# Retention's gate and stored values: two heads in one pass, 512 moving columns in place of 256

## The chip, the cores and the metric

The kernel runs on one core of one Trainium2 chip. The metric is device time in microseconds, the median of several runs. One further execution was recorded by the hardware profiler; its views are what the rows below come from.

## The reference

One decoder block over 1024 tokens of width 1024, in float32. Everything starts from one projection of the normed input, whose columns are cut into the parts that the two mixers need:

```python
h = rmsnorm(x, norm_mix)
proj = h @ w_in
(rq, rk, rv, rg, nq, kcr, vcr, ksl, vsl, kwn, vwn, ngate, ga, gb) = jnp.split(proj, split_at, axis=-1)
y_a = retention(rq, rk, rv, rg, gn_g) @ w_ret_o      # 4 heads, keys of 128, values of 256
y_b = nsa(nq, kcr, vcr, ksl, vsl, kwn, vwn, ngate, ...) @ w_nsa_o   # 8 heads, 3 branches
x = x + (sigmoid(ga) * y_a + sigmoid(gb) * y_b) @ w_out
x = x + conv_ffn(rmsnorm(x), ...)
return rmsnorm(x)
```

Inside `retention`, `rg` is the gate (`silu(g)` times the normed output, 256 columns for each of four heads) and `rv` the values (256 columns for each head).

## The kernel before

All products are float32 made of three passes: `split` writes a rounded copy (`hi`, on ScalarE, L129) and the rest (`lo`, on VectorE, L130), and `mm3` (L132 to L135) issues hi x hi, hi x lo and lo x hi into one PSUM bank. The normed input stands transposed in SBUF as `hT`, eight k slices of 128 by 1024 tokens.

`weights` (L140) loads a part of `w_in` into one of three raw buffers (`wraw`) by a transfer on SyncE's queue, and splits it into one of four pairs of buffers (`wsp`, tags `wh` and `wl`). Each buffer holds 128 x 1024 elements.

Two kinds of projection run beside attention. `stored` (L529) computes 128 channels of the merge gates for all tokens, with the weights stationary and 512 tokens of `hT` moving: 48 matmuls of 512 columns, one weight buffer. `ret_block` (L537) computes one head's 256 columns of retention's gate (`rg`) or values (`rv`), with 128 tokens of `hT` stationary and the 256 columns of the weights moving: two weight parts of four k slices each, 8 token tiles x 8 k x 3 = 192 matmuls of 256 columns. Two token tiles share a bank of PSUM, which ScalarE copies out in one instruction (`ge`, L549) and stores to scratch memory (L550).

Attention is 16 units of 128 queries and one group of heads (`unit`, L380), from the last queries to the first, each with scores, masks, exponentials, transposes and products with the values. Behind each unit the program puts one `stored` block, behind every fourth unit one gate block, and behind the last unit the value blocks of heads 0 and 1 (`SPILL_V` is 2). The framework's scheduler puts the instructions of each engine into a fixed order before the run, with the program's order as priority, and hands out buffers from the pools; so the projections fill TensorE wherever attention has nothing ready. In the trace they run ahead of the units beside which they are written. PSUM gives two banks to the projections (`mm`).

Behind this stage comes retention, head by head: query and key projections with two banks of `mm`, the stored gate loaded back (L641), for heads 0 and 1 the stored values loaded back (L660) into raw buffers, for heads 2 and 3 the values projected in place (L672 to L682). Then come the output projections, the merge and the feed-forward network, which the change does not touch.

Of the kernel before, what the change touches and what calls it, by code (L numbers as in the profile page):

```python
# [12 lines left out]
AF = mybir.ActivationFunctionType  # L13
# [5 lines left out]
P = 128  # L19
S = 1024  # L20
D = 1024
NT = S // P
KD = D // P
H_R = 4
DV = 256
# [11 lines left out]
C_RQ, C_RK, C_RV, C_RG = 0, 512, 1024, 2048  # L37
# [3 lines left out]
SPILL_V = 2  # L41
SPILL_Q = 0
# [42 lines left out]
def tile_hybrid_block(ctx: ExitStack, tc: tile.TileContext, x, norm_mix, w_in, ret_gn_g,  # L85
# [4 lines left out]
    nc = tc.nc  # L90
    x, out = x[0], out[0]
    w_in, w_ret_o, w_nsa_o, w_out = w_in[0], w_ret_o[0], w_nsa_o[0], w_out[0]
# [10 lines left out]
    def bank(tag, shape=(P, 512)):  # L103
        return psum.tile(list(shape), F32, name="ps_" + tag, tag=tag, bufs=banks[tag])


    def scratch(name, n, shape):
        return [dram.tile(list(shape), F32, name=f"{name}{i}") for i in range(n)]
# [6 lines left out]
    rv_scr = scratch("rv_scr", SPILL_V, (S, DV))  # L115
    rq_scr = scratch("rq_scr", SPILL_Q, (P, S))
    rg_scr = scratch("rg_scr", H_R, (S, DV))
# [10 lines left out]
    def split(hi, lo, src):  # L128
        nc.scalar.activation(hi, src, AF.Copy)  # L129
        nc.vector.tensor_sub(lo, src, f32(hi))  # L130

    def mm3(ps, ah, al, bh, bl, start, stop, more=False):  # L132
        nc.tensor.matmul(ps, ah, bh, start=start, stop=False, skip_group_check=more)  # L133
        nc.tensor.matmul(ps, ah, bl, start=False, stop=False, skip_group_check=more)  # L134
        return nc.tensor.matmul(ps, al, bh, start=False, stop=stop, skip_group_check=more)  # L135
# [4 lines left out]
    def weights(parts, kt=KD, raw_eng=None):  # L140

        n = sum(q[2] for q in parts)
        raw = wraw.tile([P, kt, n], F32, name="w_raw", tag="raw")
        c = 0
        for src, c0, w in parts:
            nc.sync.dma_start(raw[:, :, c:c + w],
                              src[:kt * P, c0:c0 + w].rearrange("(k p) c -> p k c", p=P))
            c += w
        wh = wsp.tile([P, kt, n], F32R, name="w_hi", tag="wh")
        wl = wsp.tile([P, kt, n], F32R, name="w_lo", tag="wl")  # L150
        split(wh, wl, raw)
        return wh, wl
# [13 lines left out]
    hT = [(hTh[k // 4][:, k % 4, :], hTl[k // 4][:, k % 4, :]) for k in range(KD)]  # L166
# [25 lines left out]
    with ExitStack() as st:  # L192
        pool = st.enter_context(tc.tile_pool(name="p0", bufs=2))
        gm = pool.tile([P, D], F32, name="gm", bufs=1)
        for t in range(NT):
# [12 lines left out]
            tok = slice(t * P, (t + 1) * P)  # L208
            for i in range(2):
                pt = bank("pt" if i else "sc", (P, 4, P))  # L210
                for j in range(4):
                    k = 4 * i + j
# [7 lines left out]
    def proj_T(c0, evac, wts=None):  # L220

        wh, wl = wts or weights([(w_in, c0, P)])
        for hf in range(2):
            ps = bank("mm")
            tok = slice(hf * 512, hf * 512 + 512)
            for k in range(KD):
                mm3(ps, wh[:, k, :], wl[:, k, :], hT[k][0][:, tok], hT[k][1][:, tok],
                    k == 0, k == KD - 1)
            evac(hf, ps)
# [299 lines left out]
    def stored(scr, c0):  # L529

        def evac(hf, ps):
            ge = npool.tile([P, 512], F32, name="ge", bufs=2)
            nc.scalar.activation(ge, ps, AF.Copy)
            nc.scalar.dma_start(scr[:, hf * 512:hf * 512 + 512], ge)
        proj_T(c0, evac)

    def ret_block(col, scr, h):  # L537
        c0 = col + h * DV
        wp = [weights([(w_in[i * 512:], c0, DV)], kt=4) for i in range(2)]
        for t in range(0, NT, 2):  # L540
            ps = bank("mm", (P, 2, DV))
            for j in range(2):
                tok = slice((t + j) * P, (t + j + 1) * P)
                for k in range(KD):
                    wh, wl = wp[k // 4]
                    mm3(ps[:, j, :], hT[k][0][:, tok], hT[k][1][:, tok],
                        wh[:, k % 4, :], wl[:, k % 4, :], k == 0, k == KD - 1)
            ge = npool.tile([P, 2, DV], F32, name="ge", bufs=2)
            nc.scalar.activation(ge, ps, AF.Copy)  # L549
            nc.scalar.dma_start(scr[h][t * P:(t + 2) * P, :].rearrange(  # L550
                "(j p) c -> p j c", p=P), ge)

    for u in range(2 * NT):
        unit(NT - 1 - u // 2, u % 2)
        scr, c0 = (ga_scr, C_GA) if u < 8 else (gb_scr, C_GB)
        stored(scr[u % 8], c0 + (u % 8) * P)
        if u % 4 == 3:
            ret_block(C_RG, rg_scr, u // 4)
    for h in range(SPILL_V):
        ret_block(C_RV, rv_scr, h)  # L560
    for h in range(SPILL_Q):
        stored(rq_scr[h], C_RQ + h * P)
    nsa_st.close()


    with ExitStack() as st:
# [32 lines left out]
        for h in range(H_R):  # L599
# [40 lines left out]
            for hf in range(2):  # L640
# [5 lines left out]
                for j in range(4):  # L646
                    c = slice(j * P, (j + 1) * P)
# [8 lines left out]
            wp = None  # L656
# [8 lines left out]
            else:  # L665
                wp = [weights([(w_in[i * 512:], C_RV + h * DV, DV)], kt=4) for i in range(2)]
            state = None
            for t in range(NT):
                hf, j = t // 4, t % 4
                c = slice(j * P, (j + 1) * P)  # L670
                tok = slice(t * P, (t + 1) * P)
                if wp:  # L672
                    ps = bank("mm")[:, 0:DV]
                    for k in range(KD):
                        wh, wl = wp[k // 4]
# [58 lines left out]
                for e in range(2):  # L734
# [5 lines left out]
                    k = 2 * h + e  # L740
# [28 lines left out]
    with ExitStack() as st:  # L769
        pool = st.enter_context(tc.tile_pool(name="mtmp", bufs=2))  # L770
        for mi in range(KD):
            wh, wl = weights([(w_ret_o, mi * P, P)])
            if mi % 4 == 0:
                mq = [half_quad("m") for _ in range(2)]
            for hf in range(2):
                tok = slice(hf * 512, hf * 512 + 512)
# [9 lines left out]
                ps = bank("sc")  # L786
# [54 lines left out]
    for ch in range(2):  # L841
        cs = slice(ch * 512, ch * 512 + 512)
        for t in (range(NT) if ch == 0 else (4, 5, 6, 7, 0, 1, 2, 3)):
            hf, j = t // 4, t % 4
            c = slice(j * P, (j + 1) * P)
            ps = bank("mm")
# [310 lines left out]
```

## Time and profile before

| | us |
|---|---|
| median of 3 runs | 1753.31 |
| lowest and highest | 1750.1, 1755.57 |
| profiled execution | 1759.76 |
| its span, first to last instruction | 1758.0 |
| TensorE matmul busy | 1707.0 (97%) |
| VectorE busy | 1118.9 (64%) |
| ScalarE busy | 801.5 (46%) |
| mean granted TensorE clock | 0.992 |

Busy time is the time in which at least one instruction of the engine was under way. Matmuls overlap, so the duration of one is longer than the distance from its start to the next one's start.

### The profile page before, as it was taken

The numbers are of one execution on the slowest core, as the hardware profiler recorded it, in microseconds if no ns is written. First come the engines' busy times: TensorE is split into PE (matmuls) and PEld (weight loads), VectorE is DVE, ScalarE is ACT, GpSimd is POOL, SyncE is SP. The second block draws the span as 40 slices with busy tenths as digits, with TensorE's granted clock in tenths as the row PEclk, the third lists the DMA queues.
The fourth block names the chain that finished last, engine by engine and source line by source line (L and its number), as shares of the span: only waits on it lengthen the run. The fifth ranks groups of instructions, "written<-read, shape, count | busy, mean of one in ns | idle before, by whom it ended". The sixth has DMA issues, their size and how long they took to land.

```text
span 1758.0 us, 24133 instructions
## 1 busy us (share of the span) xinstructions
PE 1707.0 (97%) x9005; PEld 1455.2 (83%) x9005; DVE 1118.9 (64%) x2332; ACT 801.5 (46%) x1425; POOL 87.2 (5%) x94
## 2 busy tenths in 40 slices
PE   7999999999999999999999799699999999999998
PEld 7888898888988997898878688588888888888886
DVE  6637676675766854575626326877876787765564
ACT  5435554554555754444534313443433343444442
POOL 1000000000000001222003100000000000000000
PEclk9999999999999999999999999899999999999999
DMA  6352212222122124222566612244544444686673
GB/s 212 107 148 73 64 50 84 63 72 67 58 81 67 55 85 140 85 75 82 176 216 219 227 61 85 90 136 161 177 156 144 138 171 157 227 289 217 218 219 119
DMA packets 179332, 231.56 MB, mean 132 GB/s; under 512 B 11030, under 2 KB 118030, under 8 KB 179214
## 3 DMA queue, kind: packets, MB, share of 16 engines
q1 hardware_dynamic: 143022, 167.34, 30.7%
q10 hardware_dynamic: 36192, 62.67, 9.5%
q8 instruction: 71, 1.16, 0.3%
q14 instruction: 47, 0.39, 0.1%
HBM read 163.12 MB, written 66.85 MB: 131 GB/s over the span
## 4 chain that ended last, share of the span: by engine, by line
PE 85%; DMA 7%; DVE 4%; ACT 2%; issue 1%; POOL 0%; SPq 0%; DVEq 0%; ACTq 0%; POOLq 0%
PE ps_mm L133 17%; PE ps_mm L135 17%; PE ps_mm L134 17%; PE ps_sc L135 5%; PE ps_sc L133 5%; PE ps_sc L134 5%; PE ps_pt L509 3%; DMA sga<-ga_scr 2%; PE ps_pt L135 2%; PE ps_pt L134 2%; PE ps_pt L133 2%; PE ps_sc L396 2%; PE ps_sc L395 2%; PE ps_pv L516 2%; PE ps_pv L515 2%
## 5 line engine op out<-in xcount | busy, mean ns | idle before, releaser
L133 PE MATMUL ps_mm<-hTh,w_hi 128*128 128x512 f32 x512 | 202.1, 395 | 2.8 <-DVE ql L130 2.6
L134 PE MATMUL ps_mm<-hTl,w_hi 128*128 128x512 f32 x512 | 201.9, 394 | 0.0
L135 PE MATMUL ps_mm<-hTh,w_lo 128*128 128x512 f32 x512 | 201.1, 393 | 0.0
L133 PE MATMUL ps_mm<-w_hi,hTh 128*128 128x256 f32 (+1 forms) x576 | 167.4, 291 | 2.3 <-ACT hTh L129 1.2
L135 PE MATMUL ps_mm<-w_hi,hTl 128*128 128x256 f32 (+1 forms) x576 | 167.5, 291 | 0.0
L134 PE MATMUL ps_mm<-w_lo,hTh 128*128 128x256 f32 (+1 forms) x576 | 167.1, 290 | 0.0
L130 DVE TENSOR_TENSOR w_lo<-w_raw,w_hi 128x1024 fp32r<-128x1024 f32 (+2 forms) x75 | 92.0, 1229 | 110.8 <-ACT w_hi L129 110.8
L130 DVE TENSOR_TENSOR dn<-dn_raw,dn 128x1024 fp32r<-128x1024 f32 x77 | 93.8, 1224 | 73.4 <-ACT dn L129 73.4
L129 ACT ACTIVATE dn<-dn_raw 128x1024 fp32r<-128x1024 f32 x77 | 81.4, 1060 | 115.5 <-DMA dn_raw<-p_scr 48.5
L129 ACT ACTIVATE pth<-ps_pt 128x512 fp32r<-128x512 f32 x132 | 76.6, 592 | 107.3 <-PE ps_pt L509 106.4
L129 ACT ACTIVATE w_hi<-w_raw 128x1024 fp32r<-128x1024 f32 (+2 forms) x75 | 78.5, 1047 | 81.2 <-PE ps_mm L134 48.6
L133 PEld LDWEIGHTS ps_mm<-hTh,w_hi 128*128 128x128 f32 x512 | 96.3, 188 | 22.3 <-DVE ql L130 3.0
L130 DVE TENSOR_TENSOR ptl<-ps_pt,pth 128x512 fp32r<-128x512 f32 x132 | 89.7, 687 | 39.1 <-ACT pth L129 38.8
L133 PEld LDWEIGHTS ps_mm<-w_hi,hTh 128*128 128x128 f32 x576 | 110.8, 192 | 3.9 <-ACT hTh L129 1.6
L135 PEld LDWEIGHTS ps_mm<-hTh,w_lo 128*128 128x128 f32 x512 | 96.3, 188 | 18.8 <-DVE w_lo L130 0.3
L135 PEld LDWEIGHTS ps_mm<-w_hi,hTl 128*128 128x128 f32 x576 | 110.8, 192 | 1.2 <-DVE hTl L130 0.2
L134 PEld LDWEIGHTS ps_mm<-w_lo,hTh 128*128 128x128 f32 x576 | 110.8, 192 | 1.0
L134 PEld LDWEIGHTS ps_mm<-hTl,w_hi 128*128 128x128 f32 x512 | 96.3, 188 | 18.2
L395 PE MATMUL ps_sc<-kst,q 128*128 128x512 f32 (+4 forms) x216 | 70.7, 333 | 0.0
L396 PE MATMUL ps_sc<-kst,q 128*128 128x512 f32 (+4 forms) x216 | 69.8, 329 | 0.0
L129 ACT ACTIVATE wt<-t 128x1024 fp32r<-128x1024 f32 (+1 forms) x46 | 45.3, 1013 | 52.3 <-PE ps_mm L135 47.6
L414 ACT ACTIVATE psl<-psl,nmax 128x1024 f32<-128x1024 f32 (+7 forms) x64 | 49.4, 772 | 21.6 <-DVE nmax L410 21.6
(371 smaller groups left out, 4438.6 us busy)
## 6 DMA issues: line engine op xcount, KB each, us to landing
w_raw<-in_w_in SPq DMA_DIRECT2D x48, 512.0 KB, 3.9
wu_raw<-in_w_up SPq DMA_DIRECT2D x44, 512.0 KB, 4.4
dn_raw<-p_scr SPq DMA_DIRECT2D x44, 512.0 KB, 5.0
wd_raw<-in_w_down SPq DMA_DIRECT2D x22, 512.0 KB, 5.6
p_scr<-wd_raw ACTq DMA_DIRECT2D x22, 512.0 KB, 5.2
dn_raw<-in_w_down SPq DMA_DIRECT2D x33, 256.0 KB, 4.2
g_a<-rows ACTq DMA_DIRECT2D x22, 256.0 KB, 2.1
p_scr<-rows ACTq DMA_DIRECT2D x22, 256.0 KB, 2.6
```

What stands on the lines that cost most here:

```text
L129: nc.scalar.activation(hi, src, AF.Copy)
L130: nc.vector.tensor_sub(lo, src, f32(hi))
L133: nc.tensor.matmul(ps, ah, bh, start=start, stop=False, skip_group_check=more)
L134: nc.tensor.matmul(ps, ah, bl, start=False, stop=False, skip_group_check=more)
L135: return nc.tensor.matmul(ps, al, bh, start=False, stop=stop, skip_group_check=more)
L395: nc.tensor.matmul(dst, q1[:, r, :], kap, start=True, stop=False)
L396: nc.tensor.matmul(dst, q2[:, r, :], kap, start=False, stop=True)
L414: nc.scalar.activation(p_r, p_r, AF.Exp, bias=nmax[:, br, r:r + 1], scale=-1.0, accum_out=sums[:, br, r:r + 1])
L509: nc.tensor.transpose(pt[:, r, :], pr[r][:, kt * P:(kt + 1) * P], ident)
L515: nc.tensor.matmul(pv[0:DK], v[:, 0:DK], ptl, start=False, stop=False)
L516: nc.tensor.matmul(pv, v, pth, start=False, stop=last)
```

## The change

`ret_block` becomes `ret_pair`. It takes two neighbouring heads at once: four weight parts of two k slices by 512 columns each, and for each of the eight token tiles 8 k x 3 matmuls of 512 moving columns into one bank. The copy out of PSUM keeps its size, and each head's part is stored by a transfer of its own. The gate's pairs stand behind units 5 and 11, and the two heads of values are one pair behind the last unit. `SPILL_Q` is 0, so the loop over it, which is taken out, did nothing.

```diff
-    def ret_block(col, scr, h):
-        c0 = col + h * DV
-        wp = [weights([(w_in[i * 512:], c0, DV)], kt=4) for i in range(2)]
-        for t in range(0, NT, 2):
-            ps = bank("mm", (P, 2, DV))
-            for j in range(2):
-                tok = slice((t + j) * P, (t + j + 1) * P)
-                for k in range(KD):
-                    wh, wl = wp[k // 4]
-                    mm3(ps[:, j, :], hT[k][0][:, tok], hT[k][1][:, tok],
-                        wh[:, k % 4, :], wl[:, k % 4, :], k == 0, k == KD - 1)
+    def ret_pair(col, scr, h):
+
+        wp = [weights([(w_in[i * 256:], col + h * DV, 2 * DV)], kt=2) for i in range(4)]
+        for t in range(NT):
+            tok = slice(t * P, (t + 1) * P)
+            ps = bank("mm")
+            for k in range(KD):
+                wh, wl = wp[k // 2]
+                mm3(ps, hT[k][0][:, tok], hT[k][1][:, tok], wh[:, k % 2, :], wl[:, k % 2, :],
+                    k == 0, k == KD - 1)
             ge = npool.tile([P, 2, DV], F32, name="ge", bufs=2)
-            nc.scalar.activation(ge, ps, AF.Copy)
-            nc.scalar.dma_start(scr[h][t * P:(t + 2) * P, :].rearrange(
-                "(j p) c -> p j c", p=P), ge)
+            nc.scalar.activation(ge, ps.rearrange("p (e c) -> p e c", e=2), AF.Copy)
+            for e in range(2):
+                nc.scalar.dma_start(scr[h + e][tok, :], ge[:, e])
...
-        if u % 4 == 3:
-            ret_block(C_RG, rg_scr, u // 4)
-    for h in range(SPILL_V):
-        ret_block(C_RV, rv_scr, h)
-    for h in range(SPILL_Q):
-        stored(rq_scr[h], C_RQ + h * P)
+        if u in (5, 11):
+            ret_pair(C_RG, rg_scr, 0 if u == 5 else 2)
+    ret_pair(C_RV, rv_scr, 0)
```

## Rows read from the trace of the kernel before

**Rows 1.** The page: busy time by engine, and the chain that ended last.
```profile
PE 1707.0 (97%) x9005; PEld 1455.2 (83%) x9005; DVE 1118.9 (64%) x2332; ACT 801.5 (46%) x1425; POOL 87.2 (5%) x94
...
PE 85%; DMA 7%; DVE 4%; ACT 2%; issue 1%; POOL 0%; SPq 0%; DVEq 0%; ACTq 0%; POOLq 0%
```
**Rows 2.** Stretches: length, busy time and instructions of each engine, granted clock, DMA.
```profile
core 0: us, PE busy (x) PEld busy (x) DVE busy (x) ACT busy (x) POOL busy (x), PEclk, DMA share, GB/s
145.00:300.00 155.00, 155.00 (x873) 131.73 (x872) 110.58 (x337) 83.10 (x170) 7.29 (x4) 1.00 0.22 65
300.00:450.00 150.00, 150.00 (x895) 130.22 (x893) 101.54 (x324) 77.04 (x168) 5.47 (x4) 1.00 0.24 71
450.00:600.00 150.00, 150.00 (x977) 134.29 (x976) 105.11 (x347) 89.27 (x221) 0.00 (x0) 1.00 0.21 65
600.00:661.00 61.00, 61.00 (x495) 59.37 (x494) 37.80 (x171) 34.55 (x109) 0.00 (x0) 1.00 0.23 72
661.00:700.00 39.00, 36.44 (x181) 30.38 (x180) 18.02 (x19) 16.87 (x22) 4.74 (x2) 1.00 0.53 157
```
**Rows 3.** Single lines: durations min/median/max in ns, first and last start in us.
```profile
L526 ACTq DMA_DIRECT2D o_scr<-ot x16: 366/377/482, 217.0 to 650.9; - x16
...
L549 ACT ACTIVATE ge<-ps_mm x24: 576/597/601, 228.2 to 661.3; 128x512 f32<-128x512 f32 x24
...
L550 ACTq DMA_DIRECT2D rg_scr<-ge x16: 366/366/378, 228.9 to 593.4; - x16
L550 ACTq DMA_DIRECT2D rv_scr<-ge x8: 366/366/367, 604.5 to 661.9; - x8
```
**Rows 4.** Groups of TensorE, 145 to 661 us: busy us, mean ns, idle before.
```profile
L135 PE MATMUL ps_mm<-w_hi,hTl 128*128 128x256 f32 x384 | 110.8, 289 | 0.0
L134 PE MATMUL ps_mm<-w_lo,hTh 128*128 128x256 f32 x384 | 110.4, 288 | 0.0
L133 PE MATMUL ps_mm<-w_hi,hTh 128*128 128x256 f32 x384 | 110.1, 287 | 0.0
```
**Rows 5.** TensorE in order of time: start, duration; 50 and 72 in unbroken order.
```profile
655.11 0.28 PE L134 MATMUL ps_mm<-w_lo,hTh 128*128 128x256 f32 x1
...
660.99 0.28 PE L135 MATMUL ps_mm<-w_hi,hTl 128*128 128x256 f32 x1
661.11 0.40 PE L133 MATMUL ps_mm<-hTh,w_hi 128*128 128x512 f32 x1
...
677.23 0.39 PE L135 MATMUL ps_mm<-hTh,w_lo 128*128 128x512 f32 x1
```
**Rows 6.** The same, between attention's instructions: 21 and 20 in unbroken order.
```profile
372.62 0.39 PE L133 MATMUL ps_mm<-hTh,w_hi 128*128 128x512 f32 x1
...
377.20 0.39 PE L135 MATMUL ps_mm<-hTh,w_lo 128*128 128x512 f32 x1
...
538.73 0.49 PE L135 MATMUL ps_mm<-hTh,w_lo 128*128 128x512 f32 x1
...
543.18 0.39 PE L133 MATMUL ps_mm<-hTh,w_hi 128*128 128x512 f32 x1
```
**Rows 7.** The first gate block's end, the split behind it, loads and their landing.
```profile
259.85 0.28 PE L135 MATMUL ps_mm<-w_hi,hTl 128*128 128x256 f32 x1
...
261.34 1.06 ACT L129 ACTIVATE w_hi<-w_raw 128x1024 fp32r<-128x1024 f32 x1
...
264.21 1.22 DVE L130 TENSOR_TENSOR w_lo<-w_raw,w_hi 128x1024 fp32r<-128x1024 f32 x1
...
w_raw<-in_w_in SPq DMA_DIRECT2D x48, 512.0 KB, 3.9
```
**Rows 8.** The chain of waits at retention's start, and TensorE's idle time there.
```profile
662.21 3.92 DMA w_raw<-in_w_in
...
670.89 7.09 DMA w_raw<-in_w_in
...
679.44 0.69 DVE ql L130
...
680.17 0.50 PE L133 MATMUL ps_mm<-hTh,w_hi 128*128 128x512 f32 x1 [2.56 <-DVE ql L130]
```

## The prediction

> **What bounds the kernel now.** I read the page first. TensorE is busy for 97% of the span, and the chain that ended last runs through it for 85% of its length [rows 1]. A busy TensorE is not by itself a bound, so the next view is the table of stretches. What is to be seen there: from 145 us (the first `stored` block) to 661 us (the last value block) TensorE has no idle time in any stretch, while VectorE is busy for 62 to 71% and ScalarE for 51 to 60% of each; after 661 us 2.6 us of idle time come in [rows 2]. So in the stage that the change touches, attention's chains of softmax steps run on VectorE and ScalarE, and the projection blocks fill TensorE between them. Every nanosecond that such a filler takes off TensorE's queue moves the end of the stage forward, as long as filler is left when attention is done. That is so today: the last attention unit stores its output at 650.9 us, the last value block is copied out at 661.3 us and stored at 661.9 us [rows 3].
>
> **The matmuls.** The rows for L133, L134 and L135 with 256 moving columns count 384 each in this stage: 1152 matmuls, 192 for each of the six blocks [rows 4]. After the change there are 3 pairs x 8 token tiles x 8 k x 3 = 576 with 512 columns, on the same stationary tiles. The mean durations of the groups don't give the saving, since neighbours overlap; the distance from start to start does. In the stretch without attention, 50 matmuls of 256 columns start from 655.11 to 660.99 us: 5.88/49 = 0.120 us apart. Right behind them 72 of 512 columns start from 661.11 to 677.23 us: 16.12/71 = 0.227 us apart [rows 5]. Two narrow ones cost 240 ns, one wide one 227: 13 ns, times 576 = 7.5 us. Among attention's instructions wide ones run a little slower: 21 from 372.62 to 377.20 us are 4.58/20 = 0.229 us apart, and 20 from 538.73 to 543.18 us, of which the first stands behind transposes, 4.45/19 = 0.234 us [rows 6]. Most of the pairs will run among attention, so I take 229: 240 - 229 = 11 ns x 576 = **6.3 us**. The bounds are 240 - 234 = 6 ns (3.5 us) and 13 ns (7.5 us).
>
> The narrow stream needs 0.120 us where its columns at 2.4 GHz (the granted clock is 1.00 in these stretches [rows 2]) are 256/2.4 = 107 ns, the wide one 0.227 where they are 213: about 13 ns per matmul that don't depend on its columns, and the change halves how often they are paid. The Trainium skill speaks against a gain of this size: its page "TensorE: Matmul & The Clock Gate", section "Back-to-back issue gap", puts the distance of isolated matmuls at the full clock at columns/2.4 plus only 2.5 ns. By that, an estimate, the change would save 2.5 ns x 576 = 1.4 us and could not be told from nothing. The rows decide for 13 ns, because a weight load stands before each of these matmuls.
>
> **The weights.** Twelve transfers of 512 KB and twelve splits on ScalarE and VectorE stay as many and as large, and none lies on TensorE. What changes is who holds the four weight buffers (`wsp`). A block held two, and two were left for the next blocks; a pair holds all four from its first tile to its last, since its inner loop runs through all four parts. The fourth part can only be split when the block before has finished, and the block behind a pair can only be split when the pair's last tile has passed its first two k. Each time 6 k x 3 = 18 matmuls of 0.229 us, 4.1 us, are left as cover, more where attention's matmuls stand between. The need is seen where the first gate block ends today: its last matmul starts at 259.85, the split of the buffer that it freed starts on ScalarE at 261.34 and ends on VectorE at 264.21 + 1.22 = 265.43 us, 5.6 us after the release; the two instructions alone are 1.06 + 1.22 = 2.3 us [rows 7]. So each of the six boundaries (three starts, three ends) costs from nothing up to 5.6 - 4.1 = 1.5 us, 9 us in all. I take nothing: the 5.6 us are from a moment when attention kept ScalarE and VectorE busy, and then attention also has matmuls to put into the gap; where attention is over (the end of the last pair) both engines are free and 2.3 us fit into 4.1. If that cover is gone, TensorE waits at the first matmul of the fourth part and everything behind it in its queue waits too, attention's matmuls included.
>
> **The stores.** The copy out of PSUM keeps its form (24 of 128x512, 0.6 us each), but each block of tiles is stored by two transfers in place of one: 48 issues where there were 24, each 0.366 us of ScalarE's queue [rows 3]. That is 24 x 0.366 = 8.8 us more over 516 us on an engine that is busy for about 284 of them [rows 2]. What hides it is the same filler: attention's exponentials stand behind these issues and come later by 0.37 us each time, but TensorE does other work then. Without that cover the price is at most the 8 additional issues of the last pair, 2.9 us. I take nothing. The buffer that the copy frees in PSUM isn't held by the stores.
>
> **The order.** The gate's fourth head moves from behind unit 15 to behind unit 11, beside the third. Filler is worked off in its own order, some blocks ahead of the units, so only its sum counts for the end: the 11 us by which it outlasts the last unit become some 5. Cost: nothing, as long as the units end by about 655 us.
>
> **The seam to retention.** At 677.23 us TensorE stops for 2.56 us until VectorE has copied a query half out of PSUM. The chain of waits shows what was late: a weight load of 3.92 us from 662.21, one of 7.09 us from 670.89, and then the copy at 679.44 us [rows 8]: ScalarE and VectorE stood in their queues behind splits whose data was still in flight, and by the program two of the three raw buffers held a head's stored values then. With the pair both heads' values are complete only at the end, so these loads come later. It may take the 2.56 us away or put a like wait in another place; the retention stage waits for stored values only after the first head's query and key projections, 96 matmuls x 0.227 = 21.8 us. I take nothing and keep 2.6 us to either side.
>
> **The sum.** The profiled execution took 1759.76 us (span 1758.0), 6.5 us above the median of 1753.31. 1759.76 - 6.3 = 1753.5 for that execution, and against the median 1753.31 - 6.3 = **1747.0 us**. About 0.3% (5.3 us) is what a measurement of this kernel can tell from no change: below 1748.0 is faster, above 1758.6 slower. The forecast lies just beyond that line.
>
> **The rivals.**
> - *Less saved than the streams show.* Most wide matmuls run in short groups between attention's instructions, where the slow one of the two rows, 234 ns, holds: 3.5 us, 1749.8 us, no change that can be told. For it: attention surrounds all but the last pair. Against it: a narrow matmul loses time at the same seams, and the 240 ns are from a stretch without any. The page's 2.5 ns would end in the same class.
> - *The seam's stall goes too.* 1747.0 - 2.6 = 1744.4 us. For it: the two values' loads no longer hold raw buffers while the query and key weights come. Against it: the second head's and the second half's loads then fall into the first projections.
> - *The weight buffers starve TensorE* (the other side). There are three raw buffers for a pair's four parts. If the fourth load can only start when another buffer is freed, the 3.9 us of its transfer [rows 7] come before the 2.3 us of the split: 6.2 us against a cover of 4.1, 2.1 us lost; with the queueing seen at 265 us (5.6 in place of 2.3) it is 9.5 - 4.1 = 5.4 us. At six boundaries that is 12.6 to 32 us; the smaller gives 1747.0 + 12.6 = 1759.6 us, slower. It decides against the kernel from (6.3 + 5.3)/6 = 1.9 us per boundary on. Against it: raw buffers are freed by the splits of the blocks before, of 48 x 0.229 = 11 us each, so the loads run ahead; and attention fills part of each gap.
>
> **How the numbers follow.** The forecast has a chance of 0.50, and by the spread of the three runs (1750.1 to 1755.6) and the bounds of 3.5 to 7.5 us about a quarter of it, 0.12, lies above 1748.0. Less saved, or as much saved and a few us lost at the boundaries: 0.25, all of it no change. The seam's stall gone: 0.13, faster. Starved: 0.12, of which 0.09 slower and 0.03 no change. So faster 0.38 + 0.13 = 0.51, the same 0.12 + 0.25 + 0.03 = 0.40, slower 0.09. The range reaches down to the seam's case with the upper bound of the saving and some scatter (1753.3 - 7.5 - 2.6 = 1743.2, so 1742) and up to where the boundaries take back what was saved and 2.7 us more (9 us lost): 1756.
>
> **What would show it.** In the profile after: 576 matmuls of 512 columns on L133 to L135 with `w_hi` and `w_lo` as moving tiles in this stage, 0.227 to 0.230 us from start to start; the last value block ending at about 655 us in place of 661, with TensorE's idle time before it still near nothing; the first split behind each pair ending before the pair's last matmul; and the stage from the end of the value blocks to the end as long as before. It is wrong if TensorE waits for `w_lo` at the start of a pair or behind one, if the last unit ends after the last pair, or if the retention stage behind it is longer or shorter by more than 2.6 us.

## The result, and the profile after

The changed kernel takes 1774.14 us (median of 5, 1771.36 to 1776.62), the kernel before in the same comparison 1754.94. The ratio is 1.0114, 95% interval 1.0097 to 1.0132: slower by some 20 us, where 6 us less had been forecast. The profiled execution took 1775.4 us, its span is 1773.5, 15.5 longer than before.

First the matmuls themselves, the groups of TensorE from 145 us to the end of the value pair (busy us, mean ns, idle before):

```profile
L135 PE MATMUL ps_mm<-w_hi,hTl 128*128 128x512 f32 x192 | 75.6, 395 | 0.0
L133 PE MATMUL ps_mm<-w_hi,hTh 128*128 128x512 f32 x192 | 75.4, 395 | 0.0
L134 PE MATMUL ps_mm<-w_lo,hTh 128*128 128x512 f32 x192 | 75.2, 392 | 0.0
```

These are 3 x 192 = 576 wide ones in place of [rows 4], as forecast. Then the stretches of the stage, with the columns of [rows 2]:

```profile
145.00:300.00 155.00, 155.00 (x773) 127.35 (x772) 102.50 (x311) 77.22 (x162) 7.28 (x4) 1.00 0.20 62
300.00:450.00 150.00, 150.00 (x761) 123.93 (x760) 90.26 (x270) 70.64 (x147) 4.21 (x3) 1.00 0.25 75
450.00:600.00 150.00, 150.00 (x774) 125.08 (x772) 91.69 (x291) 76.99 (x177) 1.26 (x1) 1.00 0.23 71
600.00:624.00 24.00, 24.00 (x128) 20.17 (x127) 15.39 (x52) 13.51 (x35) 0.00 (x0) 1.00 0.13 39
624.00:690.00 66.00, 52.42 (x275) 39.19 (x273) 56.41 (x246) 45.23 (x149) 0.00 (x0) 0.91 0.19 56
```

and the lines that answer to [rows 3]:

```profile
L526 ACTq DMA_DIRECT2D o_scr<-ot x16: 366/377/424, 216.3 to 687.0; - x16
...
L550 ACTq DMA_DIRECT2D rg_scr<-ge x32: 326/327/1237, 260.6 to 489.9; - x32
L550 ACTq DMA_DIRECT2D rv_scr<-ge x16: 326/370/642, 564.9 to 623.9; - x16
```

What the reader is to see: up to 624 us TensorE is as full as before. But the last value block is stored at 623.9 us in place of 661.9, and the last attention unit at 687.0 in place of 650.9. The projections, which outlasted attention by 11 us, now run out 63 us ahead of it. For those 63 us attention stands alone. TensorE idles for 66.00 - 52.42 = 13.6 us of the stretch. Of these the last 4.75 (685.25 to 690.00 us) belong to the seam shown below, so beside attention it idles for 8.8 us, most of it behind 650 us. Its granted clock is 0.91 of full over the stretch, 1.00 up to 650 us and 0.89 from there to 685.25, so part of it runs at the lower level of 1.2 GHz. VectorE shows the same from the other side. Up to 600 us it is busy for 60 to 66% of each stretch, before for 68 to 71%, because attention comes to it more slowly; afterwards it catches up (56.41 of 66.00).

The seam to retention answers to [rows 8] (TensorE, then ScalarE: start, duration, idle time and its releaser):

```profile
690.32 0.80 PE L133 MATMUL ps_mm<-hTh,w_hi 128*128 128x512 f32 x1 [5.07 <-DVE ql L130]
```
```profile
686.98 0.37 ACTq L526 DMA_DIRECT2D o_scr<-ot  x1
688.94 1.08 ACT L129 ACTIVATE qh<-ps_mm 128x512 fp32r<-128x512 f32 x2 [2.89 <-DMA o_scr<-ot]
```

TensorE now stands for 5.07 us in place of 2.56, and the cause is another: ScalarE's copy of retention's first queries waits until the last unit's output has been stored. So the end of attention is what releases the next stage. The first transposed keys of retention start at 703.3 us (before: 685.3). Of these 18 us the rest of the kernel gives 2.5 back.

**Why attention is slower.** A step of attention can be followed in the order of TensorE's queue. VectorE writes the rest of a transposed probability tile (`ptl`, L511 and L130), and the product with the values (L515) is the first matmul that needs it. In the changed kernel, beside the first pair (two tiles in one row of VectorE, the second ready at 305.30 + 1.29 = 306.59 us):

```profile
305.30 1.29 DVE L130 TENSOR_TENSOR ptl<-ps_pt,pth 128x512 fp32r<-128x512 f32 x2 [6.24 <-ACT pth L129]
```
```profile
306.76 0.40 PE L134 MATMUL ps_mm<-w_lo,hTh 128*128 128x512 f32 x1
...
310.17 0.39 PE L134 MATMUL ps_mm<-w_lo,hTh 128*128 128x512 f32 x1
310.39 0.39 PE L515 MATMUL ps_pv<-ptl,vst 128*64 128x512 f32 x1
310.62 0.39 PE L516 MATMUL ps_pv<-pth,vst 128*128 128x512 f32 x1
310.85 0.27 PE L509 MATMUL ps_pt<-ident,psl 128*128 128x128 f32 x1
310.88 0.48 PE L515 MATMUL ps_pv<-ptl,vst 128*64 128x512 f32 x1
```

The product starts at 310.88, 4.29 us after its input was ready. In between TensorE issues 19 matmuls: 16 of the pair, from 306.76 to 310.17 us and (310.17 - 306.76)/15 = 0.227 us apart, then three of attention itself. Counted in the same way over the whole first pair, the mean of 15 such products is 18.8 matmuls and 4.2 us. The trace of before has the same count and other times: 19.7 matmuls and 2.7 us (13 products) beside the first gate block, 18.9 and 4.1 us (14 products) beside the wide `stored` blocks behind it. The order of TensorE's instructions is fixed before the run, and in it a step of attention stands about 19 matmuls behind the point at which its input comes. The width of the matmuls that fill these places sets the time.

This became theory A: *what a filler costs attention is counted in matmuls; wide ones make each step wait 1.5 us longer, attention falls behind, and the projections run out before it ends.* (The expectations count only the projections among the 19, 13 to 15 in the mean.) The rivals were B, the pair's hold on all four weight buffers; C, the new places behind units 5 and 11; and D, the doubled stores on ScalarE's queue.

### The profile page after: what moved, and what is told of

Same layout as the page of the kernel before. It is cut to its first block, busy times and chain, and to the rows that moved or that the text cites. A ratio compares the mean times of both kernels' runs of the same rounds, so it can differ in the third digit from the quotient of the medians.

```text
span 1773.5 us, 22989 instructions
## 1 busy us (share of the span) xinstructions
PE 1712.7 (97%) x8429; PEld 1429.3 (81%) x8429; DVE 1118.7 (63%) x2332; ACT 800.1 (45%) x1425; POOL 86.7 (5%) x94
## 4 chain that ended last, share of the span: by engine, by line
PE 86%; DVE 5%; DMA 5%; ACT 2%; issue 1%; POOL 0%; SPq 0%; DVEq 0%; POOLq 0%; ACTq 0%
PE ps_mm L133 17%; PE ps_mm L135 17%; PE ps_mm L134 17%; PE ps_sc L135 5%; PE ps_sc L134 5%; PE ps_sc L133 5%; PE ps_pt L509 3%; PE ps_pt L135 2%; PE ps_pt L134 2%; PE ps_pt L133 2%; PE ps_sc L396 2%; PE ps_sc L395 2%; PE ps_pv L515 2%; PE ps_pv L516 2%; DMA sga<-ga_scr 2%; DMA sgb<-gb_scr 1%
## 5 line engine op out<-in xcount | busy, mean ns | idle before, releaser
L130 DVE TENSOR_TENSOR w_lo<-w_raw,w_hi 128x1024 fp32r<-128x1024 f32 (+2 forms) x75 | 92.5, 1235 | 106.1 <-ACT w_hi L129 105.7
L130 DVE TENSOR_TENSOR dn<-dn_raw,dn 128x1024 fp32r<-128x1024 f32 x77 | 94.0, 1224 | 69.6 <-ACT dn L129 69.2
L133 PE MATMUL ps_mm<-w_hi,hTh 128*128 128x512 f32 (+2 forms) x384 | 131.8, 344 | 2.4 <-ACT hTh L129 1.4
L135 PE MATMUL ps_mm<-w_hi,hTl 128*128 128x512 f32 (+2 forms) x384 | 131.5, 343 | 0.0
L134 PE MATMUL ps_mm<-w_lo,hTh 128*128 128x512 f32 (+2 forms) x384 | 131.1, 342 | 0.0
L130 DVE TENSOR_TENSOR ptl<-ps_pt,pth 128x512 fp32r<-128x512 f32 x132 | 87.7, 686 | 34.8 <-ACT pth L129 34.3
L133 PEld LDWEIGHTS ps_mm<-w_hi,hTh 128*128 128x128 f32 x384 | 73.1, 190 | 9.8 <-ACT hTh L129 1.8
L134 PEld LDWEIGHTS ps_mm<-w_lo,hTh 128*128 128x128 f32 x384 | 73.0, 190 | 7.1
L135 PEld LDWEIGHTS ps_mm<-w_hi,hTl 128*128 128x128 f32 x384 | 72.9, 190 | 7.1 <-DVE hTl L130 0.2
```

## The experiments

**e1: the width alone taken back.** Pairs, buffers, places and stores stay.

```diff
-            for k in range(KD):
-                wh, wl = wp[k // 2]
-                mm3(ps, ..., wh[:, k % 2, :], wl[:, k % 2, :], k == 0, k == KD - 1)
+            for e in range(2):
+                cs = slice(e * DV, e * DV + DV)
+                for k in range(KD):
+                    wh, wl = wp[k // 2]
+                    mm3(ps[:, cs], ..., wh[:, k % 2, cs], wl[:, k % 2, cs], k == 0, k == KD - 1)
```

> The changed kernel, but each matmul of a pair is issued as two of 256 columns (one head after the other), so that only the width goes back; pairs, buffers, places and stores stay. Theory A (each step of attention waits in TensorE's order behind some 13 to 14 projection matmuls whatever their width, so wide ones make attention slower and the projections run out before it ends): the wait between the rest of a probability tile and its product falls from 4.1 to about 2.6 us beside pairs, the last value block and the last unit end within some 12 us of each other, and the time goes back to about 1755 us (1750 to 1760). Theory B (the pair's hold on all four weight buffers) and theory C (its places behind units 5 and 11) and theory D (twice as many stores on ScalarE's queue): none of these is touched, so 1774 us, or up to 7 more for the narrow matmuls.

Measured: 1753.26 us, ratio to before 0.9981 (0.9971 to 0.9991). A step beside the first pair (second tile ready at 252.53 + 1.29 = 253.82 us, its product at 256.40):

```profile
252.53 1.29 DVE L130 TENSOR_TENSOR ptl<-ps_pt,pth 128x512 fp32r<-128x512 f32 x2 [5.99 <-ACT pth L129]
```
```profile
253.88 0.29 PE L133 MATMUL ps_mm<-w_hi,hTh 128*128 128x256 f32 x1
...
255.56 0.28 PE L135 MATMUL ps_mm<-w_hi,hTl 128*128 128x256 f32 x1
255.69 0.39 PE L515 MATMUL ps_pv<-ptl,vst 128*64 128x512 f32 x1
255.91 0.40 PE L516 MATMUL ps_pv<-pth,vst 128*128 128x512 f32 x1
256.15 0.49 PE L509 MATMUL ps_pt<-ident,psl 128*128 128x128 f32 x3
256.40 0.47 PE L515 MATMUL ps_pv<-ptl,vst 128*64 128x512 f32 x1
```

20 matmuls stand in between, and they take 2.58 us in place of 4.29; over the whole pair (27 products) the means are 18.9 and 2.6 us. The last unit ends at 645.6 and the last values at 662.8 us. The whole loss is gone with B, C and D untouched: the width (and with it the number of matmuls) is the cause, and beside narrow pairs the hold on four buffers costs no time that can be measured. The traces agree. From 145 to 624 us VectorE waits 9.1 us in all for ScalarE's half of a weight split in the kernel before, 16.0 us in e1 and 20.7 us in the changed kernel (4.8 at most at once). The changed kernel's 4.7 us over e1 are far from the 41 us by which its last unit ends later.

**e2: the places alone.** The kernel before, with two one-head blocks behind units 5 and 11 each.

```diff
-        if u % 4 == 3:
-            ret_block(C_RG, rg_scr, u // 4)
+        if u in (5, 11):
+            for h in range(2):
+                ret_block(C_RG, rg_scr, (0 if u == 5 else 2) + h)
```

> The kernel before, with its one-head blocks of 256 columns, but written at the places of the pairs: heads 0 and 1 behind unit 5, heads 2 and 3 behind unit 11, values at the end. Theory A: 1755 us as before, within 4. Theory C (places): about 1774 us. Theories B and D: 1755 us.

Measured: 1754.94 us, ratio 0.9995 (0.9985 to 1.0005). C is out.

**e3: one store for a tile of both heads.** The pair's heads share a scratch tensor of 1024 x 2 x 256.

```diff
-            for e in range(2):
-                nc.scalar.dma_start(scr[h + e][tok, :], ge[:, e])
+            nc.scalar.dma_start(scr[h // 2][tok], ge)
```

> The changed kernel, but the two heads of a pair share one scratch tensor and each token tile is stored by one transfer, so ScalarE issues 24 stores again. Theory D: the time falls by a good part of the 19 us, to 1765 us or less. Theory A, B or C: 1774 us, within 4.

Measured: 1775.61 us, ratio 1.0102 (1.0085 to 1.0119), no gain. D is out.

**e4: more to fill the gap with.** The queries of two retention heads join the projections beside attention.

```diff
-SPILL_Q = 0
+SPILL_Q = 2
...
     ret_pair(C_RV, rv_scr, 0)
+    for h in range(SPILL_Q):
+        stored(rq_scr[h], C_RQ + h * P)
```

> The changed kernel with two more projection blocks behind the last pair: the queries of retention's heads 0 and 1, computed beside attention and stored, then loaded back (SPILL_Q 2 in place of 0). That moves 96 wide matmuls, 22 us of TensorE, from retention into the stage. Theory A (TensorE idles at the end of attention because the projections have run out): the idle time of some 24 us beside the last units is filled and the time falls by about 15 to 22 us, to 1752 to 1759 us. Theory B (buffers) or D (stores): the last units are slow for a reason that more projections do not mend, and the moved blocks delay them further: 1765 to 1775 us.

Measured: 1778.05 us, ratio 1.0120 (1.0105 to 1.0135). The expectation failed: nothing was won. The stretches with the added blocks, behind them, and at retention's start:

```profile
600.00:661.00 61.00, 61.00 (x326) 51.40 (x325) 39.21 (x139) 34.74 (x92) 0.00 (x0) 1.00 0.24 77
661.00:705.00 44.00, 35.46 (x179) 26.75 (x178) 33.75 (x161) 26.88 (x96) 0.00 (x0) 0.85 0.10 28
705.00:740.00 35.00, 28.06 (x125) 22.88 (x126) 25.98 (x46) 22.88 (x34) 6.29 (x5) 0.75 0.62 183
```

The added blocks do fill TensorE up to 661 us. But they are wide, attention's last unit now ends at 703.4 us in place of 687.0, and behind them the same gap opens (44.00 - 35.46 = 8.5 us idle, 6.9 more in the next stretch, at a clock of 0.85 and 0.75). Retention starts without two of the projections that covered its first steps. Here the gap that wide filler made wasn't mended by more wide filler; narrow blocks were not tried in its place.

**e5: the `stored` blocks of the kernel before made narrow too.** `proj_T` gets a switch that runs each bank as two accumulations of 256 tokens; `stored` sets it.

```diff
-            for k in range(KD):
-                mm3(ps, wh[:, k, :], wl[:, k, :], hT[k][0][:, tok], hT[k][1][:, tok], ...)
+            for n0 in ((0, 256) if narrow else (0,)):
+                nw = 256 if narrow else 512
+                for k in range(KD):
+                    mm3(ps[:, n0:n0 + nw], wh[:, k, :], wl[:, k, :],
+                        hT[k][0][:, hf * 512 + n0:hf * 512 + n0 + nw], ...)
```

> The kernel before, with the matmuls of the stored gate projections (stored) cut from 512 columns to two of 256 as well, so that every projection beside attention is narrow. Theory A (a fixed count of projection matmuls stands before each step of attention): the wait between a probability tile's rest and its product is about 2.6 us throughout, the last unit ends 40 to 60 us earlier than the last value block (at some 600 us), TensorE never idles in the stage, and the time rises only by the narrow matmuls themselves: 768 pairs x 11 ns = 8 us, to about 1764 us (1759 to 1768). Rival (narrow projections are simply what this schedule likes, and attention's pace decides the time): the time falls below 1750 us.

Measured: 1762.69 us, ratio 1.0032 (1.0022 to 1.0042). The last unit ends at 603.7 us, 47 us earlier than before, the values at 669.9, and the time rises by the price of the narrow matmuls, 7 us where 8 were expected. Attention that ends still earlier before its cover is worth nothing here.

**e6, e7, e8: some pairs wide.** The pair of e1 with a switch: the first gate pair alone, the value pair alone, or both gate pairs wide.

```diff
-            for e in range(2):
-                cs = slice(e * DV, e * DV + DV)
+            for c0 in ((0,) if wide else (0, DV)):
+                cs = slice(c0, c0 + (2 * DV if wide else DV))
```

> Pairs as in the changed kernel, but only the first gate pair (behind unit 5) has wide matmuls, the other two are cut into 256 columns. Theory A: a third of the units' delay of 41 us, so the last unit ends at about 660 us, at the same time as the last value block (659 us): nothing idles or next to nothing, and 2 us of matmuls are saved against the all-narrow pairs: 1750 to 1755 us. Rival (any wide pair costs some 6 us, a third of the 19): 1759 us.

> The same with only the last pair, the values, wide. Theory A: units 9 to 15 run beside it, so they end some 10 to 14 us later than with all pairs narrow, at 656 to 660 us, about when the values end: 1750 to 1756 us. Rival (any wide pair costs a third of the 19 us): 1759 us.

> Both gate pairs wide, the values narrow. Theory A: the last unit ends some 27 us later than with all pairs narrow, at about 673 us, 16 us after the last value block; of that some 6 to 8 us are idle, so 1756 to 1762 us. Rival (each wide pair costs a third of the 19 us): 1766 us.

Measured: e6 1758.73 us, ratio 1.0016 (1.0008 to 1.0025), 4 us above what was expected. e7 1751.78 us, ratio 0.9978 (0.9967 to 0.9988), as expected; the lowest ratio of the study, though its interval overlaps with those of e1, e9 and e10. e8 1765.48 us, ratio 1.0054 (1.0041 to 1.0067), 3.5 us above. That each wide pair costs a third of the loss would fit e6 and e8 but not e7: the wide pair that stands early, beside the longest units, holds attention back by 672.4 - 645.6 = 27 us, the one that stands last by 14.

**e9, e10: wide pairs, narrow `stored` blocks.** The changed kernel, and `stored` narrow by e5's switch: all 16 blocks, or the second eight.

> The changed kernel with its wide pairs, but the stored projections (16 blocks) cut to 256 columns. Theory A, in its sharper form (attention's steps stand a fixed count of projection matmuls apart, so what covers attention is the number of these matmuls, not their time): there are 1536 + 576 = 2112 of them, more than the 1920 of the kernel before, so the last unit ends before the last value block and TensorE doesn't idle; the time is that of before less 6.3 us for the pairs plus 8.4 us for the narrow blocks, 1758 us (1753 to 1762). Rival (wide matmuls in the pairs cost some 19 us by themselves): 1774 to 1783 us.

> The same, but only the second eight stored blocks (the gate of the second mixer) are narrow: 384 + 768 + 576 = 1728 matmuls, as many as with one wide pair in three. Theory A: between the two kernels with one wide pair, 1751 to 1760 us, the last unit ending at about the same time as the last value block or up to 13 us behind it. Rival (wide pairs cost by themselves): 1774 to 1779 us.

Measured: e9 1752.91 us, ratio 0.9987 (0.9977 to 0.9996); e10 1752.64 us, ratio 0.9986 (0.9976 to 0.9995). All three wide pairs are in both, and the 20 us are gone: the loss isn't a property of the pair but of the width of all that stands before attention's steps, the `stored` blocks included. e9 is slightly faster than its two prices (-6.3 and +8.4) say; that wasn't followed up.

**e11: a third width.** The matmuls of all pairs in four parts of 128 columns, one run.

```diff
+            for c0 in range(0, 2 * DV, 128):
+                cs = slice(c0, c0 + 128)
...
```

> The changed kernel with each matmul of a pair cut into four of 128 columns (2304 in place of 576), one look. Theory A: between a probability tile's rest and its product stand again some 13 to 14 projection matmuls beside the pairs, so the wait falls to about 1 us there (13.5 x 0.066 = 0.9 us if these narrow ones follow each other as the wide ones do, 13 ns over their columns); the last unit ends before 640 us and the value blocks last longer than before: 2304 x 0.066 = 152 us in place of 138, about 1769 us. Rival (the wait is a time of 2.6 to 4 us that attention's other engines set): the wait stays at 2.6 us.

Measured: 1866.49 us, one run. A step beside the first pair, its tile ready at 388.67 + 0.69 = 389.36 us:

```profile
388.67 0.69 DVE L130 TENSOR_TENSOR ptl<-ps_pt,pth 128x512 fp32r<-128x512 f32 x1 [2.73 <-ACT pth L129]
```
```profile
389.42 0.27 PE L133 MATMUL ps_mm<-w_hi,hTh 128*128 128x128 f32 x1
...
391.43 0.27 PE L133 MATMUL ps_mm<-w_hi,hTh 128*128 128x128 f32 x1
391.54 0.40 PE L515 MATMUL ps_pv<-ptl,vst 128*64 128x512 f32 x1
```

Again 19 matmuls, the same count at a third width; a fixed wait of 2.6 us, as the rival has it, would have some 2.6/0.112 = 23 (an estimate). But they stand (391.43 - 389.42)/18 = 0.112 us apart, not 0.066, so the wait is 2.2 us and not 0.9. That is close to the 2.6 us of e1, so the run is a weak test between the two, and the kernel is 112 us slower than before. The last unit ends at 701.9 us although more matmuls than ever stand beside attention. The trace shows why. The twelfth unit is stored at 583.8 us, and then VectorE does nothing until 623 us:

```profile
623.02 2.36 DVE L130 TENSOR_TENSOR w_lo<-w_raw,w_hi 128x1024 fp32r<-128x1024 f32 x2 [39.25 <-ACT w_hi L129]
```

The next instruction in VectorE's queue is a weight split, and it waits for ScalarE's half of that split, which comes only when the second gate pair on TensorE is done; meanwhile, from 583.8 to 621.9 us, TensorE runs 341 matmuls of the pair and none of attention. So the count is right for the single step, but the number of filler matmuls alone does not give the end of attention: here the pair's hold on the four buffers (B) stops it for 39 us, where the longest such wait in the changed kernel is 4.8 us.

Where attention and the projections ended (the last store of each, us), with the ratio to before:

| kernel | last unit | last projection | ratio |
|---|---|---|---|
| e9, pairs wide, stored narrow | 623.9 | 663.3 | 0.9987 |
| e1, pairs narrow | 645.6 | 662.8 | 0.9981 |
| e7, value pair wide | 659.7 | 660.6 | 0.9978 |
| e10, pairs wide, half of stored narrow | 665.1 | 659.5 | 0.9986 |
| e6, first pair wide | 672.4 | 659.4 | 1.0016 |
| e8, gate pairs wide | 680.4 | 640.6 | 1.0054 |
| changed, all wide | 687.0 | 623.9 | 1.0114 |

In this table the ratio is 0.998 to 0.999 with attention first or no more than 6 us behind. From there on it rises with the distance between the two ends (13, 40 and 63 us).

## Why the prediction was wrong

**The bound** was read rightly: TensorE sets the stage's end as long as filler is left when attention is done. That condition is what broke.

**The matmuls** were sized rightly: 576 of them, 0.227 us apart among attention's instructions (the row above), where 0.229 was taken. How much of the 6.3 us was saved could be seen by itself for one pair only: the value pair is the last work in e7, and its last store stands at 660.6 us where that of e1 stands at 662.8, although the last unit ends later. The difference is 2.2 us, a third of 6.3 is 2.1.

**The order** is the step that failed: "Filler is worked off in its own order, some blocks ahead of the units, so only its sum counts for the end", and with it "Cost: nothing, as long as the units end by about 655 us". It took attention's pace as given and the cover as a sum of time. The units ended at 687.0 us. Filler and attention share one queue in a fixed order, and a wider filler matmul lengthens the wait of every step of attention behind it: 4.2 us in place of 2.6 beside a pair. The trace of before held it: its wide `stored` stretches have the 4.1 us wait and its narrow blocks the 2.7 us one. The prediction took the distance of matmuls from such a stretch [rows 6] and never looked at what waits behind them.

**The weights, the stores, the places** cost nothing, as taken: e1, e3 and e2 show each by itself, and TensorE has no idle time from 145 to 624 us in the changed kernel, so no pair's start or end made it wait. The prediction counted its 5.6 us of a split from the start of the block's last matmul; from its end, 259.85 + 0.28 = 260.13 us, they are 5.3. In e11 the hold did cost, but in VectorE's queue, where the prediction had not looked.

**The seam** moved the other way: 5.07 us idle in place of 2.56, because retention's first copy waits for the last unit's store, which now comes last. The program opens retention's buffers when it has closed attention's; that the copy waits for this reason was not tested.

**The rivals.** The slower rival had the right sign, for a wrong reason and with 1759.6 us too small a time. None of the rivals had attention slowed by the filler. What would have shown the failure was named ("if the last unit ends after the last pair"), but with no chance of its own.

What the 20 us consist of is shown only in part: 8.8 us of idle time beside attention, 2.5 us more at the seam, and the lower clock behind 650 us (0.89 to the end of attention and 0.93 from 690.32 to 720 us; before, 1.00 from 661 to 700 us [rows 2]). How much the lower clock cost by itself was not measured. Why the fixed order puts about 19 matmuls before a step was not tried. Over the whole stage the count holds only roughly: when the tenth unit is stored, 1311 projection matmuls of the trace have started in the changed kernel (at 607 us), 1423 in the one before (564 us), 1414 in e1 (547 us), but 1669 in e5 (509 us).

## What to carry to other kernels

Where two streams share an in-order queue, look at how long the dependent stream's steps wait behind the other's instructions, and in what unit: here a step waits a count of matmuls, so making each one larger slows the dependent stream even when it saves time in sum. Filler must outlast what it covers: compare the two ends first, and make filler wide only as far as that margin allows. Here the last pair alone did no harm; that it gains anything over narrow pairs (0.9978 against 0.9981) is not shown. Adding more of the same filler to the gap that its size had made did not close it (e4).

## What was not expected of the hardware

Matmuls of 128 columns follow each other at 0.112 us, hardly closer than those of 256 at 0.120 [rows 5], while 512 take 0.227. So the 13 ns over the columns' own time that the prediction found at 256 and 512 columns are no constant: at 128 columns they would be 0.112 - 128/2.4 ns = 59 ns. A floor near 0.11 us per matmul with its own weight load would agree with all three widths, but no run here has these matmuls without the load, so it isn't shown that the load is the cause. The Trainium skill, "TensorE: Matmul & The Clock Gate", section "LDWEIGHTS (loading the stationary operand)", puts a weight load at its columns/1.2, by which 128 columns take an estimated 107 ns; the 0.112 us of e11 are just above that. The Trainium skill's rule of 2.5 ns per isolated matmul (same page, section "Back-to-back issue gap"), weighed in the prediction, would give 56 ns at this width, and no stretch here shows that.
